# Second norm's scaling and modulation on ScalarE, key transposes after the next projection

## Chip, cores and metric

The kernel runs on one core of one Trainium2 chip. The metric is device time of one execution in microseconds (us), the median of several runs. Engines: PE is TensorE (PEld its weight loads), DVE is VectorE, ACT is ScalarE, POOL is GpSimd, SP issues the DMAs.

## What is computed

One layer of a decoder trunk over 1024 tokens of 1024 channels, in float32:

```python
mod = silu(c) @ w_ada + b_ada                  # sh1, sc1, g1, sh2, sc2, g2
h   = rms_norm(x, g_pre_mix) * (1 + sc1) + sh1
proj = h @ w_in                                # u, v, q, k, val, qi, ki, wi
y_a = spatial_gating(gelu(u), gelu(v), ...)    # 4 groups x 128, chunks of 128 positions
q, k, q_idx, k_idx = partial_rope(...)
y_b = dsa_attention(q, k, val, q_idx, k_idx, wi)   # top 256 keys of an indexer, softmax
o   = concat(rms_norm(y_a), rms_norm(y_b)) @ w_out
x   = x + g1 * rms_norm(o, g_post_mix)
h2  = rms_norm(x, g_pre_ffn) * (1 + sc2) + sh2     # the second norm
f   = square(relu(h2 @ w_ff1)) @ w_ff2
x   = x + g2 * rms_norm(f, g_post_ffn)
```

## The kernel before

The 1024 tokens are worked in 8 blocks of 128 (`j`), in two halves of 512 (`hh = j // 4`). Every matrix product is made of three passes: each float32 operand is split into a high part (rounded to the PE's fast float32 format, written by ACT) and a low part (source minus high part, by DVE or POOL), and high x high, high x low and low x high are summed in PSUM.

The order of instructions on each engine is not written by hand. The program is traced in source order, which gives each instruction a priority; `stage(n)` sets the priority of what follows. A planner that runs ahead of time with its own estimates of durations then takes, for each engine, the first instruction in priority that it reckons ready, and fixes that order. On the chip each engine runs its list strictly in this order and waits at semaphores. Tiles come from pools: tiles with one tag share `bufs` buffers, and a tile's first writer waits until the last reader of the tile that had the buffer before.

**Keys, end of stage 1 and stage 2 (L349 to L373).** For each block `j`: `proj` multiplies the block's normed rows by the 328 columns wC1 (keys, index key, index weights, values): 24 matmuls into one PSUM bank. Blocks 0 and 1 use tag `mm`, blocks 2 and 3 `lg`, blocks 4 to 7 `mm` again, which has two buffers. ACT copies the result out: `kv` (L361, each head twice), `WI` (L362), `VV` (L364); the bank is free after that. `rope` rotates `kv` on POOL (L314 to L317). PE transposes the three heads (`dup_T`, L322) into a `tr` bank; ACT copies them to `KS` and `KI` (L370, L371), and DVE subtracts there to get low parts (L372, L373). `kv` has two buffers. `modulate(1, ...)` (L287 to L294) makes the normed rows of blocks 4 to 7 out of channels x tokens tiles, at `j == 1` and `j == 2`: DVE L291, ACT L293 (high part), POOL or DVE L294 (low part). Stage 3 begins with `qi_proj` (L421), 512 columns wide, with the weights `wC0`, which take over buffers of `wC1` as block 7's projection has read them.

**Second norm, stage 8 (L912 to L931, `h2_block` L875).** For each block: load `x` (4 buffers) and the first half of `o`; `oproj` (24 matmuls, L795 to L797) into an `mm` bank; ACT squares it with a sum (L921); DVE and POOL make the reciprocal root (`rstd_of`: DVE L98, POOL power L99); DVE scales by it and the gate row (L924, L925), adds `x` (L926); the result is stored. Then the second norm: ACT squares the row with a sum (L928), `rstd_of` again, DVE scales the row (L930), and `h2_block` transposes its 8 channel blocks in two halves of four (L886). The first half is modulated (times `G2`, plus `SH2`, one number per channel) by four ACT instructions (L889), the second half by one DVE product (L892) and one POOL sum (L894). For the first 512 tokens two `split`s follow (ACT L863, DVE L864). For the others come differences for a fast matrix product of seven instead of eight sub-products: `t1` (DVE L903, L904), POOL L907 and L909, and four splits into `HB[1]`, `TT3` and `TT2`. Stage 9 then multiplies by `w_ff1`: the products of its first two weight tiles need `HB[0]` alone at first (L1012 and before), and then `T1` and `B22`, which are the two halves of `HB[1]` and need all four of its blocks (L1020, L1021; the matmuls are at L974 to L976).

Of the kernel before, what the change touches and what calls it, by code (L numbers as in the profile page):

```python
# [9 lines left out]
F32 = mybir.dt.float32  # L10
# [5 lines left out]
AF = mybir.ActivationFunctionType  # L16
OP = mybir.AluOpType
PSUM = bass.MemoryType.PSUM

P = 128  # L20
# [17 lines left out]
def trunk(ctx, tc, x, c, positions, w_ada, b_ada, g_pre_mix, w_in, g_sgu_v, w_spatial, b_spatial,  # L38
          g_out_sgu, g_out_attn, w_out, g_post_mix, g_pre_ffn, w_ff1, w_ff2, g_post_ffn, out):
    nc = tc.nc  # L40
    V, A, G, T = nc.vector, nc.scalar, nc.gpsimd, nc.tensor
# [5 lines left out]
    def nm(s):  # L47
        uid[0] += 1
        return f"{s}_{uid[0]}"
# [13 lines left out]
    def p_mm():  # L63
        return ps.tile([P, 512], F32, tag="mm", name=nm("mm"))

    def p_tr():
        return ps.tile([P, 512], F32, tag="tr", name=nm("tr"), bufs=3)
# [4 lines left out]
    def ct(shape, dt, name):  # L72
        return cst.tile(shape, dt, tag=name, name=name)

    def push(name, side="left"):
        st = ExitStack()
        return st, st.enter_context(tc.tile_pool(name=name, bufs=1, side=side, reuse_waits="tile"))

    def stage(n):
        tc.cur_priority = n * 100000  # L80
# [15 lines left out]
    def rstd_of(dst, ss, n):  # L96
        w = ss.shape[-1]
        V.tensor_scalar(dst, ss, 1.0 / n, EPS, op0=OP.mult, op1=OP.add)  # L98
        G.tensor_tensor(dst, dst, mhalf[:, :w], op=OP.pow)  # L99

    mid_stack, mid = push("mid")
    KS = mid.tile([P, 2, S], F32R, name="KS")
# [8 lines left out]
    KI = kp.tile([P, S], F32R, name="KI")  # L111
    t0_stack, t0 = push("t0")
# [174 lines left out]
    def modulate(hh, ks=range(KD), tok=slice(0, 512)):  # L287
        for k in ks:
            g, sh = G1[:, k:k + 1], SH1[:, k:k + 1]
            f = t0.tile([P, 512], F32, tag="hf", name=nm("hf"), bufs=2)[:, :tok.stop - tok.start]  # L290
            V.tensor_scalar(f, xT[hh][:, k, tok], g, sh, op0=OP.mult, op1=OP.add)  # L291
            hi = hT[hh][:, 0, k, tok]
            A.activation(hi, xT[hh][:, k, tok], AF.Identity, scale=g, bias=sh)  # L293
            (G if k % 4 in (1, 3) else V).tensor_tensor(hT[hh][:, 1, k, tok], f, hi.bitcast(F32), op=OP.subtract)  # L294

    def proj(p, j, wt, n, ks=range(KD)):
        h, t = hT[j // 4], (j % 4) * P
        first = None
        for k in ks:
            lh, ll = h[:, 0, k, t:t + P], h[:, 1, k, t:t + P]  # L300
            mm = T.matmul(p[:, :n], lh, wt[k][:, 0, :n], start=k == 0, stop=False)  # L301
            first = first or mm
            T.matmul(p[:, :n], lh, wt[k][:, 1, :n], start=False, stop=False)  # L303
            T.matmul(p[:, :n], ll, wt[k][:, 0, :n], start=False, stop=k == KD - 1)  # L304
        return first
# [13 lines left out]
    def dup_T(p, t, heads):  # L319

        for i, h in enumerate(heads):
            T.transpose(p[:, i * P:(i + 1) * P], t[:, h].rearrange("p w e -> p (w e)"), ident)  # L322
# [23 lines left out]
        pre_norm(j)  # L346
    stage(2)
    modulate(0, range(4, KD))
    for j in range(NB):  # L349
        if j == 1:  # L350
            modulate(1, tok=slice(0, 256))
        if j == 2:
            modulate(1, tok=slice(256, 512))
        if j < 4:
            p = p1[j]
            proj(p, j, wC1, 328, range(4, KD))
        else:
            p = p_mm()
            proj(p, j, wC1, 328)
        kv = t0.tile([P, 3, 2, 64], F32, tag="kv", name=nm("kv"), bufs=2)  # L360
        A.activation(kv, p[:, :192].rearrange("p (h e) -> p h e", h=3)[:, :, None, :].to_broadcast([P, 3, 2, 64]), AF.Copy)  # L361
        A.activation(WI[:, j], p[:, 192:200], AF.Copy, scale=float(8.0 ** -0.5) * 0.125)  # L362
        vv = p[:, 200:328].rearrange("p (h e) -> p h e", h=2)
        A.activation(VV[:, j], vv, AF.Copy)  # L364
        rope(kv.rearrange("p h w e -> p (h w e)"), j, 6, kp)
        pt = p_tr()
        dup_T(pt, kv, range(3))
        s = slice(j * P, (j + 1) * P)
        pt3 = pt[:, :384].rearrange("p (h t) -> p h t", h=3)
        A.activation(KS[:, :, s], pt3[:, 0:2], AF.Copy)  # L370
        A.activation(KI[:, s], pt3[:, 2], AF.Copy)  # L371
        V.tensor_tensor(KS[64:128, :, s], pt3[64:128, 0:2], KS[64:128, :, s].bitcast(F32), op=OP.subtract)  # L372
        V.tensor_tensor(KI[64:128, s], pt3[64:128, 2], KI[64:128, s].bitcast(F32), op=OP.subtract)  # L373

    def q_stack(pool, q, grp, qs):

# [98 lines left out]
    G2 = ct([P, 8], F32, "G2")  # L475
    SH2 = ct([P, 8], F32, "SH2")
# [56 lines left out]
    for cc in range(2):  # L533
        wt = w_chunk(w_in, [(0, C_U + 256 * cc, 256), (256, C_V + 256 * cc, 256)])
        for j in range(NB):
            p = p_mm()
# [38 lines left out]
    for b in range(2, NB):  # L575
        f, i = ct([P, 14], F32, f"self{b}"), ct([P, 3], I32, f"seli{b}")
# [285 lines left out]
    def split(hi, lo, src, eng):  # L862
        A.activation(hi, src, AF.Copy)  # L863
        eng.tensor_tensor(lo, src, hi.bitcast(F32), op=OP.subtract)  # L864
# [7 lines left out]
    rs2 = ct([P, NB], F32, "rs2")  # L872
    HB = {}

    def h2_block(j, y):  # L875
        t = (j % 4) * P
        hh = j // 4
        if hh not in HB:
            HB[hh] = hm.tile([P, 2, KD, 512], F32R, tag="hm", name=nm("hb"))
        f = y.rearrange("p (k t) -> p k t", k=KD)  # L880
        for half in range(2):
            ks = slice(half * 4, half * 4 + 4)
            p = p_tr()
            for i in range(4):
                k = half * 4 + i
                T.transpose(p[:, i * P:(i + 1) * P], y[:, k * P:(k + 1) * P], ident)  # L886
            if half == 0:
                for i in range(4):
                    A.activation(f[:, i, :], p[:, i * P:(i + 1) * P], AF.Identity, scale=G2[:, i:i + 1],  # L889
                                 bias=SH2[:, i:i + 1])  # L890
            else:
                V.tensor_tensor(f[:, ks], p.rearrange("p (k t) -> p k t", k=4), G2[:, ks, None].to_broadcast([P, 4, P]),  # L892
                                op=OP.mult)
                G.tensor_tensor(f[:, ks], f[:, ks], SH2[:, ks, None].to_broadcast([P, 4, P]), op=OP.add)  # L894
        tk = slice(t, t + P)
        if hh == 0:
            for half in range(2):
                ks = slice(half * 4, half * 4 + 4)
                split(HB[0][:, 0, ks, tk], HB[0][:, 1, ks, tk], f[:, ks], V)
            return  # L900
        b11 = [HB[0][:, q, 0:4, tk].bitcast(F32) for q in range(2)]
        t1 = l2.tile([P, 4, P], F32, tag="t1", name=nm("t1"), bufs=1)
        V.tensor_tensor(t1, f[:, 0:4], b11[0], op=OP.subtract)  # L903
        V.tensor_tensor(t1, t1, b11[1], op=OP.subtract)  # L904
        split(HB[1][:, 0, 0:4, tk], HB[1][:, 1, 0:4, tk], t1, V)
        split(HB[1][:, 0, 4:8, tk], HB[1][:, 1, 4:8, tk], f[:, 4:8], V)
        G.tensor_tensor(f[:, 0:4], f[:, 4:8], f[:, 0:4], op=OP.subtract)  # L907
        split(TT3[:, 0, :, tk], TT3[:, 1, :, tk], f[:, 0:4], V)
        G.tensor_tensor(f[:, 4:8], f[:, 4:8], t1, op=OP.subtract)  # L909
        split(TT2[:, 0, :, tk], TT2[:, 1, :, tk], f[:, 4:8], V)  # L910

    wo = w_chunk(w_out, [(0, 512, 512)], gout)  # L912
    for j in range(NB):
        xt = l2.tile([P, D], F32, tag="x", name=nm("x"), bufs=4)
        nc.sync.dma_start(xt, x2d[j * P:(j + 1) * P, :])
        o0 = l2.tile([P, 512], F32, tag="o0", name=nm("o0"), bufs=2)
        nc.sync.dma_start(o0, o0_dram[j * P:(j + 1) * P, :])
        p = p_mm()
        oproj(p, j, wo)
        x1 = l2.tile([P, D], F32, tag="x1", name=nm("x1"), bufs=2)  # L920
        A.activation(x1[:, 0:512], p, AF.Square, accum_out=sso[:, j, 1:2])  # L921
        V.tensor_tensor(rso[:, j:j + 1], sso[:, j, 0:1], sso[:, j, 1:2], op=OP.add)
        rstd_of(rso[:, j:j + 1], rso[:, j:j + 1], D)
        V.scalar_tensor_tensor(x1[:, 0:512], o0, rso[:, j:j + 1], g1b[:, 0:512], op0=OP.mult, op1=OP.mult)  # L924
        V.scalar_tensor_tensor(x1[:, 512:], p, rso[:, j:j + 1], g1b[:, 512:], op0=OP.mult, op1=OP.mult)  # L925
        V.tensor_tensor(x1, x1, xt, op=OP.add)  # L926
        nc.sync.dma_start(out2d[j * P:(j + 1) * P, :], x1)
        A.activation(xt, x1, AF.Square, accum_out=ss2[:, j:j + 1])  # L928
        rstd_of(rs2[:, j:j + 1], ss2[:, j:j + 1], D)
        V.tensor_scalar(xt, x1, rs2[:, j:j + 1], None, op0=OP.mult)  # L930
        h2_block(j, xt)  # L931
    l2_stack.close()

# [69 lines left out]
    for pi in range(NF):  # L1003
        raw = load_w1(pi)
        AW[pi] = {key: wsplit(raw[key], G) for key in raw}
        for fi in range(2):
            p = bank()
# [3 lines left out]
            p = bank()  # L1011
            product(p, AW[pi][fi, 1], B21)  # L1012
            f = F0[pi, fi] = dtile()
# [3 lines left out]
    for pi in range(NF):  # L1017
        for fi in range(2):
            p = bank()
            product(p, AW[pi][fi, 0], T1, stop=False)  # L1020
            product(p, AW[pi][fi, 1], B22, start=False)  # L1021
            f = part[pi, fi]
# [7 lines left out]
    for k in range(4):  # L1030
        t = fd.tile([P, 512], F32, tag="s", name=nm("t4"), bufs=4)
# [245 lines left out]
```

## Time and profile before

| | |
|---|---|
| median of 3 runs | 1256.06 us (1253.9 to 1257.73) |
| profiled execution | 1255.87 us, of which span 1254.1 us |
| mean granted TensorE clock | 0.961 of full |
| PE / DVE / ACT / POOL busy | 93% / 70% / 53% / 18% |

The span goes from the first to the last instruction of the profiled execution; the rest of its time lies around it. Times within the rows further down count from the span's start. A busy share is the share of a stretch in which the engine has an instruction under way. Matmuls are pipelined: the distance of two starts, not the duration, is what one costs.

### The profile page before, as it was taken

To read this page: it belongs to the slowest core of one execution; us is meant where nothing else is said; L and a number is where in the kernel's file an instruction comes from. 1 tells how busy PE (TensorE), PEld (TensorE's weight loads), DVE (VectorE), ACT (ScalarE), POOL (GpSimd) and SP (SyncE) were. 2 spreads that over 40 slices of the span, in tenths; PEclk is the share of its full clock that TensorE was granted. 3 is DMA by queue.
4 is the path that set the end of the run, shared out by engine and by line. 5 is a ranking of instruction groups with operands and counts; after the bars stand their busy time and mean duration, and the time that the engine had idled before them with its cause. 6 is when DMAs were issued, how large, how long until landed. Compare 5 with 4: busy or idle time off the path is not lost.

```text
span 1254.1 us, 16871 instructions
## 1 busy us (share of the span) xinstructions
PE 1169.4 (93%) x5785; PEld 987.7 (79%) x5785; DVE 876.2 (70%) x1782; ACT 661.9 (53%) x1402; POOL 222.9 (18%) x312
## 2 busy tenths in 40 slices
PE   4889979899699999899899999999999999999997
PEld 4877757688588998887677888888887888888886
DVE  6833998957697566627998875656648756876568
ACT  4544668772167755635525465555544554445452
POOL 3574702544300000013620000000000000000001
PEclk9889978899798999999999999999999999999999
DMA  9421200201002044446315753435459355533335
GB/s 344 146 67 43 68 1 18 85 22 55 1 9 68 26 152 160 168 136 226 126 43 185 269 192 127 161 126 175 151 201 353 118 177 182 198 98 101 102 95 207
DMA packets 80239, 162.41 MB, mean 130 GB/s; under 512 B 7724, under 2 KB 32920, under 8 KB 80152
## 3 DMA queue, kind: packets, MB, share of 16 engines
q1 hardware_dynamic: 80136, 161.33, 38.1%
q8 instruction: 45, 0.74, 0.2%
q14 instruction: 42, 0.34, 0.1%
q10 hardware_dynamic: 16, 0.00, 0.0%
HBM read 119.36 MB, written 41.94 MB: 129 GB/s over the span
## 4 chain that ended last, share of the span: by engine, by line
PE 60%; DVE 7%; issue 3%; DMA 1%; POOL 1%; ACT 1%; DVEq 0%; POOLq 0%; SPq 0%; ACTq 0%
PE lg L1157 9%; PE tr L1157 9%; PE mm L1157 6%; PE mm L743 5%; PE lg L974 3%; PE lg L975 3%; PE lg L976 3%; PE tr L974 3%; PE tr L976 3%; PE tr L975 3%; PE tr L757 2%; PE lg L718 2%; PE mm L974 2%; PE mm L975 2%; PE mm L976 2%
## 5 line engine op out<-in xcount | busy, mean ns | idle before, releaser
L863 ACT ACTIVATE w<-rx 128x512 fp32r<-128x512 f32 x112 | 70.6, 630 | 147.3 <-PE lg L1157 66.7
L1157 PE MATMUL tr<-w,w 128*128 128x512 f32 x504 | 133.8, 391 | 2.4 <-DVE w L864 2.4
L1157 PE MATMUL lg<-w,w 128*128 128x512 f32 x504 | 133.7, 391 | 0.0
L301 PE MATMUL mm<-w,hT 128*128 128x512 f32 (+1 forms) x288 | 113.2, 394 | 7.9 <-ACT hT L293 3.4
L864 DVE TENSOR_TENSOR w<-rx,w 128x512 fp32r<-128x512 f32 x112 | 77.4, 691 | 60.5 <-ACT w L863 60.3
L1193 POOL TENSOR_TENSOR rsf<-rsf,mhalf 128x1 f32<-128x1 f32 x8 | 6.0, 751 | 604.4 <-DVE rsf L1192 604.4
L1157 PEld LDWEIGHTS tr<-w,w 128*128 128x128 f32 x504 | 95.0, 189 | 22.5 <-DVE w L864 2.8
L304 PE MATMUL mm<-w,hT 128*128 128x512 f32 (+1 forms) x288 | 111.4, 388 | 1.0 <-POOL hT L294 1.0
L303 PE MATMUL mm<-w,hT 128*128 128x512 f32 (+1 forms) x288 | 111.7, 388 | 0.0
L1157 PEld LDWEIGHTS lg<-w,w 128*128 128x128 f32 x504 | 95.1, 189 | 19.7
L1157 PE MATMUL mm<-w,w 128*128 128x512 f32 x336 | 94.5, 392 | 0.0
L743 PEld LDWEIGHTS mm<-VV,pT 128*128 128x128 f32 x576 | 75.3, 199 | 4.5 <-ACT pT L738 2.5
L743 PE MATMUL mm<-VV,pT 128*128 128x64 f32 x576 | 76.3, 277 | 1.0 <-ACT pT L738 1.0
L1157 PEld LDWEIGHTS mm<-w,w 128*128 128x128 f32 x336 | 63.4, 189 | 13.2
L301 PEld LDWEIGHTS mm<-w,hT 128*128 128x128 f32 x288 | 56.2, 195 | 18.6 <-ACT hT L293 3.6
L864 DVE TENSOR_TENSOR w<-b,w 128x512 fp32r<-128x512 f32 x96 | 65.9, 687 | 3.6 <-ACT w L863 3.6
L864 DVE TENSOR_TENSOR w<-s,w 128x512 fp32r<-128x512 f32 x56 | 38.2, 690 | 37.6 <-ACT w L863 37.4
L304 PEld LDWEIGHTS mm<-w,hT 128*128 128x128 f32 x288 | 55.7, 194 | 10.4 <-POOL hT L294 1.3
L863 ACT ACTIVATE w<-b 128x512 fp32r<-128x512 f32 x96 | 59.3, 618 | 7.1 <-DMA b<-in_w_ff_dram 7.1
L303 PEld LDWEIGHTS mm<-w,hT 128*128 128x128 f32 x288 | 56.2, 195 | 8.5
L718 PE MATMUL lg<-KS,qs 128*128 128x512 f32 (+5 forms) x192 | 53.3, 388 | 10.2 <-DVE qs L383 8.8
L722 ACT ACTIVATE L<-L,mxs 128x128 f32<-128x128 f32 (+7 forms) x64 | 49.2, 770 | 20.4 <-DVE mxs L719 20.4
(357 smaller groups left out, 2988.6 us busy)
## 6 DMA issues: line engine op xcount, KB each, us to landing
rx<-x_scratch SPq DMA_DIRECT2D x56, 512.0 KB, 3.6
x_scratch<-d SPq DMA_DIRECT2D x108, 256.0 KB, 3.0
ada<-in_w_ada_dram SPq DMA_DIRECT2D x48, 512.0 KB, 5.7
raw<-in_w_ff_dram SPq DMA_DIRECT2D x32, 512.0 KB, 3.9
b<-in_w_ff_dram SPq DMA_DIRECT2D x32, 512.0 KB, 4.4
x<-in_x_dram SPq DMA_DIRECT2D x16, 512.0 KB, 5.5
raw<-in_w_in_dram SPq DMA_DIRECT2D x8, 512.0 KB, 3.7
raw<-in_w_in_dram SPq DMA_DIRECT2D x16, 256.0 KB, 2.9
```

What stands on the lines that cost most here:

```text
L301: mm = T.matmul(p[:, :n], lh, wt[k][:, 0, :n], start=k == 0, stop=False)
L303: T.matmul(p[:, :n], lh, wt[k][:, 1, :n], start=False, stop=False)
L304: T.matmul(p[:, :n], ll, wt[k][:, 0, :n], start=False, stop=k == KD - 1)
L718: T.matmul(pl, QS[b, grp][:, q, h4 * P:(h4 + 1) * P], KS[:, grp, c0:c0 + cw], start=q == 0, stop=q == 1)
L722: ex = A.activation(L, L, AF.Exp, scale=-1.0, bias=top, accum_out=sms[:, b, h:h + 1])
L743: mm = T.matmul(po[:, o:o + 64], e[:, (si * 2 + h2) * P:(si * 2 + h2 + 1) * P], VV[:, s0 + si, grp], start=first, stop=pair == 1 and s0 + ...
L863: A.activation(hi, src, AF.Copy)
L864: eng.tensor_tensor(lo, src, hi.bitcast(F32), op=OP.subtract)
L974: ms.append(T.matmul(p, a[:, 0, k], b[:, 0, k], start=start and k == 0, stop=False, skip_group_check=more))
L975: ms.append(T.matmul(p, a[:, 0, k], b[:, 1, k], start=False, stop=False, skip_group_check=more))
L976: ms.append(T.matmul(p, a[:, 1, k], b[:, 0, k], start=False, stop=stop and k == 3, skip_group_check=more))
L1157: ms.append(T.matmul(p, x[:, qa, t * P:(t + 1) * P], y[:, qb], start=start and n == 0, stop=stop and n == 2, skip_group_check=more))
```

## The change

The keys' transposes of a block, with the copies and subtractions behind them, go into a function `keys_T` that is called one block later: after the next block's projection, copies and rotation. `kv` gets a third buffer. In the second norm, the row's scaling goes from DVE to ACT, and the second half of the channels is modulated like the first, by four ACT instructions, in place of the DVE product and the POOL sum.

```diff
+    keys = []
+
+    def keys_T(j, kv):
+
+        pt = p_tr()
+        dup_T(pt, kv, range(3))
+        s = slice(j * P, (j + 1) * P)
+        pt3 = pt[:, :384].rearrange("p (h t) -> p h t", h=3)
+        A.activation(KS[:, :, s], pt3[:, 0:2], AF.Copy)
+        A.activation(KI[:, s], pt3[:, 2], AF.Copy)
+        V.tensor_tensor(KS[64:128, :, s], pt3[64:128, 0:2], KS[64:128, :, s].bitcast(F32), op=OP.subtract)
+        V.tensor_tensor(KI[64:128, s], pt3[64:128, 2], KI[64:128, s].bitcast(F32), op=OP.subtract)
+
     for j in range(NB):
...
-        kv = t0.tile([P, 3, 2, 64], F32, tag="kv", name=nm("kv"), bufs=2)
+        kv = t0.tile([P, 3, 2, 64], F32, tag="kv", name=nm("kv"), bufs=3)
...
         rope(kv.rearrange("p h w e -> p (h w e)"), j, 6, kp)
-        pt = p_tr()
-        dup_T(pt, kv, range(3))
...
+        if keys:
+            keys_T(*keys.pop(0))
+        keys.append((j, kv))
+    keys_T(*keys.pop(0))
...
-            if half == 0:
-                for i in range(4):
-                    A.activation(f[:, i, :], p[:, i * P:(i + 1) * P], AF.Identity, scale=G2[:, i:i + 1],
-                                 bias=SH2[:, i:i + 1])
-            else:
-                V.tensor_tensor(f[:, ks], p.rearrange("p (k t) -> p k t", k=4), G2[:, ks, None].to_broadcast([P, 4, P]),
-                                op=OP.mult)
-                G.tensor_tensor(f[:, ks], f[:, ks], SH2[:, ks, None].to_broadcast([P, 4, P]), op=OP.add)
+            for i in range(4):
+                k = half * 4 + i
+                A.activation(f[:, k, :], p[:, i * P:(i + 1) * P], AF.Identity, scale=G2[:, k:k + 1],
+                             bias=SH2[:, k:k + 1])
...
-        V.tensor_scalar(xt, x1, rs2[:, j:j + 1], None, op0=OP.mult)
+        A.activation(xt, x1, AF.Copy, scale=rs2[:, j:j + 1])
         h2_block(j, xt)
```

## Rows read from the trace of the kernel before

**Rows 1.** The page: busy time of each engine, and the chain by engine.
```profile
PE 1169.4 (93%) x5785; PEld 987.7 (79%) x5785; DVE 876.2 (70%) x1782; ACT 661.9 (53%) x1402; POOL 222.9 (18%) x312
...
PE 60%; DVE 7%; issue 3%; DMA 1%; POOL 1%; ACT 1%; DVEq 0%; POOLq 0%; SPq 0%; ACTq 0%
```

**Rows 2.** Busy by stretch: length, then busy (xcount) PE, PEld, DVE, ACT, POOL; clock, DMA.
```profile
65.00:80.00 15.00, 9.79 (x50) 9.15 (x49) 7.82 (x17) 4.44 (x19) 8.80 (x19) 0.77 0.12 35
...
150.00:330.00 180.00, 163.04 (x715) 132.79 (x714) 139.03 (x445) 108.47 (x305) 65.00 (x103) 0.91 0.11 32
...
640.00:1254.00 614.00, 602.69 (x2646) 495.79 (x2645) 422.99 (x680) 296.40 (x530) 5.98 (x8) 0.99 0.49 166
```

**Rows 3.** The same view for the second norm's stage and its end.
```profile
606.00:640.10 34.10, 26.20 (x112) 21.03 (x111) 33.18 (x39) 19.09 (x39) 21.76 (x17) 0.88 0.22 78
...
566.70:640.10 73.40, 64.29 (x297) 52.27 (x296) 64.00 (x92) 42.87 (x93) 41.15 (x35) 0.94 0.39 137
564.70:640.10 75.40, 66.29 (x306) 53.96 (x305) 65.97 (x93) 43.29 (x95) 41.15 (x35) 0.94 0.41 145
```

**Rows 4.** PE in order of time: start, us, instruction, [idle before <-releaser].
```profile
61.95 0.49 PE L322 MATMUL tr<-ident,kv 128*128 128x128 f32 x3
...
71.35 0.55 PE L322 MATMUL tr<-ident,kv 128*128 128x128 f32 x3 [3.94 <-POOL kv L317]
73.16 0.64 PE L301 MATMUL mm<-w,hT 128*128 128x328 f32 x1 [1.26 <-ACT VV L364]
73.60 0.48 PE L303 MATMUL mm<-w,hT 128*128 128x328 f32 x1
73.87 0.48 PE L304 MATMUL mm<-w,hT 128*128 128x328 f32 x1
...
80.48 0.42 PE L301 MATMUL mm<-w,hT 128*128 128x328 f32 x1 [0.34 <-ACT VV L364]
80.73 0.31 PE L303 MATMUL mm<-w,hT 128*128 128x328 f32 x1
80.88 0.31 PE L304 MATMUL mm<-w,hT 128*128 128x328 f32 x1
...
84.18 0.40 PE L301 MATMUL mm<-w,hT 128*128 128x512 f32 x1
```

**Rows 5.** ACT in order of time, the copies of keys and of block 4.
```profile
71.93 0.38 ACT L370 ACTIVATE KS<-tr 128x256 fp32r<-128x256 f32 x1 [4.05 <-PE tr L322]
...
72.37 0.50 ACT L361 ACTIVATE kv<-mm 128x384 f32<-128x384 f32 x1
```

**Rows 6.** POOL in order of time: end of block 2's rotation, last low half.
```profile
71.01 0.28 POOL L317 TENSOR_TENSOR kv<-ra,rb 128x48 f32<-128x48 f32 x1
...
72.51 0.73 POOL L294 TENSOR_TENSOR hT<-hf,hT 128x256 fp32r<-128x256 f32 x1 [0.23 <-DVE hf L291]
```

**Rows 7.** PE in order of time, its two long waits in the second norm.
```profile
622.99 3.80 PE L886 MATMUL tr<-ident,x 128*128 128x128 f32 x16 [4.99 <-DVE x L930]
...
638.67 0.80 PE L974 MATMUL lg<-hb,w 128*128 128x512 f32 x1 [2.66 <-ACT hb L863]
```

**Rows 8.** Single lines, whole run: xcount, ns min/median/max, first and last start.
```profile
L930 DVE TENSOR_SCALAR x<-x,rs x8: 741/754/1773, 570.7 to 623.4; 128x1024 f32<-128x1024 f32 x8
L892 DVE TENSOR_TENSOR x<-tr,G x8: 678/679/686, 576.6 to 627.5; 128x512 f32<-128x512 f32 x8
L894 POOL TENSOR_TENSOR x<-x,SH x8: 1041/1481/1952, 577.4 to 630.1; 128x512 f32<-128x512 f32 x8
L904 DVE TENSOR_TENSOR t<-t,hb x4: 678/1215/1778, 613.2 to 636.2; 128x512 f32<-128x512 f32 x4
L928 ACT ACTIVATE x<-x x8: 1047/1062/1065, 566.7 to 615.6; 128x1024 f32<-128x1024 f32 x8
```

**Rows 9.** ACT in order of time: eight modulations of 128 channels in a row.
```profile
574.85 2.91 ACT L889 ACTIVATE x<-tr,SH,G 128x128 f32<-128x128 f32 x8 [0.61 <-PE tr L886]
```

**Rows 10.** DVE in order of time: block 1's scaling behind POOL's power.
```profile
571.52 0.15 DVE L98 TENSOR_SCALAR rs<-ss 128x1 f32<-128x1 f32 x1
572.33 0.75 DVE L930 TENSOR_SCALAR x<-x,rs 128x1024 f32<-128x1024 f32 x1 [0.65 <-POOL rs L99]
```

More of the change, by code (lines that the diff above doesn't have):

```diff
@@ L365, in trunk @@
         rope(kv.rearrange("p h w e -> p (h w e)"), j, 6, kp)
-        pt = p_tr()
-        dup_T(pt, kv, range(3))
[L368 to L373, printed above, removed]
+        if keys:
+            keys_T(*keys.pop(0))
+        keys.append((j, kv))
+    keys_T(*keys.pop(0))
     def q_stack(pool, q, grp, qs):
```

## Prediction

> **What bounds the kernel now.** Read first the busy shares and the chain that ended last: TensorE (PE) is busy 93% of the span and carries 60% of the chain; VectorE (DVE) is at 70%, ScalarE (ACT) at 53% [rows 1]. The reader is to see that a gain can only come where PE stands still or runs at its lower clock, and that ACT has room on average; an average says nothing of a stage. So the second view is busy time by stretch. From 640 us to the end PE works 602.7 of 614 us and nothing of the change lies there [rows 2]: whatever is saved earlier arrives at the end whole, unless the stage between takes it back. From 150 to 330 us PE is at 163 and DVE at 139 of 180 us [rows 2], all of it behind the projections of stage 3, so a shift goes through, if the planner keeps its order.
>
> The change touches two stretches. **65 to 80 us**: PE is busy 9.8 of 15 us at a granted clock of 0.77 [rows 2]. **566 to 640 us** (second norm): after 606 us DVE is busy 33.2 of 34.1 us, ACT 19.1, PE 26.2 [rows 3]. There PE waits 4.99 us for the scaled rows of L930, a DVE instruction, and 2.66 us for the last split tile [rows 7]. In this stage DVE is the bound.
>
> **The keys.** The transposes of a block's keys already stand far behind later projections: those of block 0 run at 61.95 us, with block 4's projection on both sides [rows 4], since the planner places by readiness. The new order in the source alone moves little. What binds is a buffer: with two kv tiles, block 4's copy out of PSUM (L361, 72.37 us) may not run before block 2's keys are transposed (71.35 us) [rows 4, 5], and block 6's projection may not have its bank before that copy. The third kv buffer breaks this tie. It adds no instruction and takes 1.5 KB per partition of a pool that is closed after the stage; no DMA is moved, and nothing is moved past a queue that issues one.
>
> Removed for certain are the two waits for a bank behind ACT's copy of VV: 1.26 us at 73.16 and 0.34 us at 80.48 [rows 4]: 1.6 us. Open is the stall ahead of them, 3.94 us until POOL has rotated block 2's keys (L317, done at 71.29 us) [rows 4, 6], and what it leaves behind: matmuls at a distance of 0.27 us (73.60, 73.87), at full clock 0.15 us (80.73, 80.88) [rows 4], some 20 of them, 2.4 us. The granted clock falls from 2.4 to 1.2 GHz behind the stall. ACT is idle from 67.88 us (71.93 less 4.05 [rows 5]); block 4 could be copied out then, in the 0.8 us from 72.37 to 73.16, so that block 6 starts at 68.7 us, if the planner puts it ahead of the transposes that come ready at 71.29 us. It can't end before the last low half of its rows (L294 on POOL, 72.51 + 0.73 us [rows 6]), 73.3 us; block 7 takes 24 x 0.15 = 3.6 us more, and stage 3 starts at about 77.4 us instead of 84.18 [rows 4]: 6.8 us at the most. If the planner keeps the transposes ahead, 1.6 us is all. Below that it may fall to nothing where other work then stands in front. I take **2.5 us**: the certain part and a quarter of the stall. Before, the order was forced by the buffer, so it doesn't tell which one the planner prefers; the low end is nearer as PE needs the transposes first wherever both look ready.
>
> **The second norm.** Removed from DVE: 8 scalings (L930, 0.75 us median, up to 1.77) and 8 products (L892, 0.68 us); from POOL: 8 sums (L894, 1.48 us) [rows 8]. That is 8 x 0.75 + 8 x 0.68 = 11.4 us of DVE and 11.8 us of POOL. DVE also gets back part of what it loses while POOL works: the same 128x512 subtraction L904 takes 0.68 to 1.78 us [rows 8]. Added to ACT: 8 scalings of 128x1024, nearest row the Square L928 of the same shape, 1.06 us [rows 8], 8.5 us; and 32 activations of 128x128 at 2.91 / 8 = 0.364 us each (L889 [rows 9]), 11.6 us. ACT: 20.1 us more.
>
> The sum goes by the stage. ACT has 42.9 us of work in the 73.4 us from 566.7 to 640.1; then it has 63.0 us. DVE falls from 66.0 us (of 75.4) to 54.6 [rows 3]. So the bound passes from DVE to ACT, and the question is how full ACT can be: the stage keeps its length at 63.0 / 73.4 = 86%. DVE as the bound came to 66.0 / 75.4 = 87.5% over the stage and to 97% at its end [rows 3]. ACT at 87.5% needs 72.0 us (1.4 us gained), at 97% 64.9 us (8.5 us). I take 90%, 70.0 us, **3.4 us** gained: ACT has work of several blocks to choose from, as DVE had, but each block now comes to it three times (square, scaling, modulation), and the planner's order is fixed beforehand. What is late next is again the last block's split tile ahead of PE's restart at 638.67 us [rows 7]. The path of one block is hardly longer: the scaling 1.06 for 0.75 us, the second half's modulation 4 x 0.364 = 1.46 us for 0.68 + 1.48 us and a handover [rows 8, 9]. Cover: POOL's and DVE's removed work hides nothing; the added ACT work lies beside PE's oproj and the first products of stage 9, and without that cover costs its 20.1 us less DVE's 11.4, 8.7 us.
>
> The trace has an ACT instruction with two per-channel operands at 0.364 us for 128 columns [rows 9], and DVE with POOL at 2.16 us for 512. The Trainium skill (ScalarE: Activation LUTs, Rules for kernel authors) speaks against the edit: multiplications and additions belong on VectorE, not on ScalarE. By that rule alone the sum would be a loss; for the scaling the rows agree (1.06 against 0.75 us), for the modulation they don't, as half of the work it replaces is POOL's. The skill (SBUF — State Buffer, Who interferes with whom) also has a DVE instruction with two SBUF inputs contend with a GpSimd one that reads SBUF; the spread of L904 [rows 8] agrees, and this adds DVE time back that I don't count.
>
> **Sum.** The profiled execution took 1255.87 us (span 1254.1 and 1.8 around it), 0.2 under the median. 1255.87 - 2.5 - 3.4 = 1250.0 us.
>
> **Rivals.**
> *ACT becomes a worse bound than DVE was (slower).* Each scaling needs the square of its own block, the small sum on DVE and POOL's power. DVE itself waited 0.65 us there after a 0.15 us instruction (L930 at 572.33 us [rows 10]), 0.8 us in all. If the planner puts L930 straight behind L928 on ACT, with copies and splits queued behind it, 8 x 0.8 = 6.4 us of ACT go idle: 69.4 us at 87.5% is 79.3 us, 5.9 us longer than 73.4. With the certain 1.6 us of the keys 1260.2 us, without it 1261.8. It decides where ACT is less than 86% full. For it: ACT sits in the in-order chain three times. Against: blocks overlap, and DVE did reach 97%. Chance 0.19.
> *Nothing to be measured.* The keys give only the bank waits, ACT reaches 87.5%: 1255.87 - 1.6 - 1.4 = 1252.9 us. For it: the new bound is nearly as high as the old. This holds too where the reordered keys do nothing, as they already stand behind later projections. Chance 0.31.
> *Both ends good.* Block 6 goes ahead of the transposes, 6.8 us, and ACT takes 3.4 to 8.5 us less: 1240.6 to 1245.7 us. Chance 0.12.
>
> **How the numbers follow.** The forecast, 0.38, reaches from 1246 to 1252 us. A measurement of this kernel can tell about 0.3%, 3.8 us, from no change: faster ends at 1252.3, slower begins at 1259.8 us. Faster: 0.38 less a small part, and the good end, 0.48. Same: the second rival and that part, 0.33. Slower: the first, 0.19. A new plan also shuffles orders that have nothing to do with the change, which is why no case is a point. The range of 8 in 10 goes from 1243 to 1260 us; left out are half of the good end and most of the slower case beyond 1260.
>
> **What would show it.** Keys: kv of block 4 on ACT ahead of block 2's KS copy; no 1.26 us wait for VV; first 512-wide matmul of stage 3 at 77 to 82.5 us instead of 84.18. If PE still stands some 4 us before a kv transpose, the low end held. Norm: ACT 86% full or more from 567 us to PE's restart, DVE under 80%; the restart 3 to 4 us earlier when counted from the start of stage 8. The prediction is wrong if ACT waits on POOL's power (L99) at each scaling, if PE waits for a bank of oproj behind ACT, or if the stretch between 100 and 560 us changes length by more than 2 us.

## The result and the profile after

| | before | after |
|---|---|---|
| median of 5 runs | 1254.46 us (1253.6 to 1257.73) | 1246.09 us (1243.53 to 1247.74) |
| profiled execution, of which span | 1255.87 us, 1254.1 us | 1243.53 us, 1241.8 us |
| mean granted TensorE clock | 0.961 | 0.971 |

The changed kernel takes 0.9924 of the time before, 95% interval 0.9905 to 0.9943: 8.4 us less by the medians, 9.5 us by this ratio, where 1250.0 us (5.9 less than the profiled execution) was forecast and 1243 to 1260 given as the range. The profiled execution of after is the fastest of its five, so the two traces differ by 12.3 us at their ends; the size of the gain is taken from the medians, the traces say where it lies.

The page of the kernel after, busy time of each engine and the chain by engine, to be held against [rows 1]:

```profile
PE 1161.0 (93%) x5785; PEld 979.4 (79%) x5785; DVE 861.9 (69%) x1766; ACT 680.6 (55%) x1442; POOL 212.0 (17%) x304
...
PE 59%; DVE 6%; issue 3%; ACT 3%; DMA 2%; POOL 0%; SPq 0%; DVEq 0%; POOLq 0%; ACTq 0%
```

ACT works 18.7 us more, DVE 14.3 and POOL 10.9 us less. ACT's share of the chain rises from 1% to 3%. PE's busy time falls too, by 8.4 us with the same 5785 matmuls: part of what was saved is matmuls at the lower clock, and not idle time.

PE of the kernel after in order of time: the start, the duration, the instruction, and the idle time before it with its releaser. The rows up to 77.15 us answer to [rows 4], the rest to [rows 7]:

```profile
60.71 0.49 PE L322 MATMUL tr<-ident,kv 128*128 128x128 f32 x3
...
68.56 0.55 PE L322 MATMUL tr<-ident,kv 128*128 128x128 f32 x3 [2.24 <-POOL kv L317]
68.88 0.41 PE L301 MATMUL mm<-w,hT 128*128 128x328 f32 x1
69.14 0.31 PE L303 MATMUL mm<-w,hT 128*128 128x328 f32 x1
69.29 0.31 PE L304 MATMUL mm<-w,hT 128*128 128x328 f32 x1
...
77.15 0.39 PE L301 MATMUL mm<-w,hT 128*128 128x512 f32 x1
...
610.78 1.09 PE L895 MATMUL tr<-ident,x 128*128 128x128 f32 x8 [0.45 <-ACT x L935]
...
612.82 0.65 PE L895 MATMUL tr<-ident,x 128*128 128x128 f32 x4 [0.95 <-ACT x L935]
...
614.74 0.66 PE L895 MATMUL tr<-ident,x 128*128 128x128 f32 x4 [1.26 <-ACT x L898]
...
616.65 0.80 PE L979 MATMUL tr<-hb,w 128*128 128x512 f32 x1 [1.26 <-ACT x L898]
...
628.18 0.50 PE L979 MATMUL lg<-hb,w 128*128 128x512 f32 x1 [1.68 <-ACT hb L872]
```

The third set of transposes, block 2's, is still the one that PE waits for, and still for POOL's rotation, but 2.24 us instead of 3.94. Block 6's projection (L301 at 68.88) follows at once: the 1.26 us wait for a bank is gone. Its matmuls stand 0.15 us apart (69.14, 69.29) instead of 0.27. The first 512-wide matmul comes at 77.15 instead of 84.18 us. In the second norm the 4.99 us wait for DVE's scaled row has turned into four small waits for ACT, 3.9 us together, and the restart on the split tile comes at 628.18 instead of 638.67 us.

Busy time by stretch: length, then busy us (count) of PE, PEld, DVE, ACT, POOL, then the granted clock, DMA share and GB/s. First of the kernel before, two pieces of the keys' stretch and stage 8 from its first square to PE's restart:

```profile
70.00:75.00 5.00, 2.39 (x10) 2.15 (x11) 2.97 (x9) 1.18 (x5) 4.54 (x13) 0.68 0.00 0
75.00:80.00 5.00, 5.00 (x25) 4.87 (x24) 0.16 (x1) 0.75 (x3) 0.14 (x1) 0.64 0.00 0
...
559.50:638.70 79.20, 70.09 (x327) 57.13 (x325) 65.63 (x95) 43.21 (x97) 41.02 (x37) 0.96 0.45 160
```

The same view of the kernel after; the last row begins at the first square of L933:

```profile
65.00:80.00 15.00, 12.76 (x83) 11.92 (x82) 9.38 (x22) 9.46 (x34) 14.46 (x27) 1.00 0.25 71
...
551.20:628.20 77.00, 69.36 (x327) 56.42 (x325) 48.67 (x79) 60.94 (x137) 29.86 (x29) 0.98 0.47 164
558.10:628.20 70.10, 62.47 (x297) 50.69 (x295) 45.63 (x74) 59.55 (x132) 29.31 (x27) 0.98 0.42 145
```

From 65 to 80 us PE is busy 12.8 of 15 us instead of 9.8 [rows 2]. From 70 to 80 us the granted clock was 0.68 and 0.64, the mean of pieces at 1.2 and at 2.4 GHz; after, it is 1.00 from 65 to 80 us. Stage 8 is 2.2 us shorter (79.2 to 77.0), with DVE's work down by 17.0 us and ACT's up by 17.7: the fullest engine beside PE is now ACT.

Counted along the trace, after is ahead of before by 7.0 us at the start of stage 3, by 8.3 us at the first square of stage 8 (551.21 for 559.54 us), by 10.5 us at PE's restart and by 10.0 us at the first product with TT (655.65 for 665.62 us). Of the first 7.0 us, 1.2 are there before block 0's transposes already (60.71 for 61.95 us). This mark lies between 60.71 and 63.45 us in all kernels below and goes with no edit, so the keys account for 5.8 us in this pair of traces.

### The profile page after: what moved, and what is told of

Read it like the earlier page. It is cut to its first block, busy times and chain, and to the rows that moved or that the text cites. A ratio compares the mean times of both kernels' runs of the same rounds, so it can differ in the third digit from the quotient of the medians.

```text
span 1241.8 us, 16873 instructions
## 1 busy us (share of the span) xinstructions
PE 1161.0 (93%) x5785; PEld 979.4 (79%) x5785; DVE 861.9 (69%) x1766; ACT 680.6 (55%) x1442; POOL 212.0 (17%) x304
## 4 chain that ended last, share of the span: by engine, by line
PE 59%; DVE 6%; issue 3%; ACT 3%; DMA 2%; POOL 0%; SPq 0%; DVEq 0%; POOLq 0%; ACTq 0%
PE tr L1162 8%; PE lg L1162 8%; PE mm L1162 5%; PE mm L752 4%; PE lg L980 3%; PE lg L981 3%; PE lg L979 3%; PE tr L981 3%; PE tr L980 3%; PE tr L979 3%; PE tr L766 2%; PE lg L727 2%; PE mm L981 2%; PE mm L980 2%; PE mm L979 2%
## 5 line engine op out<-in xcount | busy, mean ns | idle before, releaser
L301 PE MATMUL mm<-w,hT 128*128 128x512 f32 (+1 forms) x288 | 112.0, 390 | 4.4 <-ACT hT L293 3.7
L301 PEld LDWEIGHTS mm<-w,hT 128*128 128x128 f32 x288 | 55.2, 192 | 15.1 <-ACT hT L293 3.9
L304 PEld LDWEIGHTS mm<-w,hT 128*128 128x128 f32 x288 | 54.9, 191 | 10.0 <-POOL hT L294 0.6
L303 PEld LDWEIGHTS mm<-w,hT 128*128 128x128 f32 x288 | 55.3, 192 | 8.5
```

## The experiments

The theories. *The buffer*: what binds the keys is the two kv tiles, and the order in the source does nothing. Rival: the order is needed as well, or alone. *The stage's bound*: the second norm gains because DVE, with POOL, was its bound and hands work to ACT; rivals: only one of the two edits gives the gain, or POOL's sums are what cost the time and it doesn't matter where the work goes.

**The two halves of the change, each alone.** keys_only takes the diff without its two edits in stage 8, norm_only these two alone.

> The keys' part alone (keys_T one block later, third kv buffer); second norm as before. Theory A: the keys' part carries most of the gain, since stage 3 began 7.0 us earlier in the changed kernel (77.15 against 84.18 us) and stage 8 8.3 us earlier: 6 to 8 us faster than before, first 512-wide matmul at about 77 us. Rival B: the two parts share the gain as predicted, keys 2.5 us: 1.6 to 3 us faster. Rival C: most of what stands at stage 8 is a shuffled plan between, then the start of stage 3 moves by 7 us but the end by less than 4.

> The second norm's part alone (scaling and all modulation on ACT); keys as before. Theory A: 1.5 to 2.5 us faster, since from the first square of oproj to PE's restart on the split tiles the changed kernel took 77.0 us and before 79.1; with ACT 85% full in that stretch. Prediction's term: 3.4 us. Rival: nothing or a loss, the whole gain being that of the keys.

Measured: keys_only 0.9943 (0.9929 to 0.9956), 7.2 us less; norm_only 0.9973 (0.996 to 0.9986), 3.4 us less. Together 10.6 us, where both at once gave 9.5 (0.9924): additive as far as the intervals can tell, so no sign that one half takes the other's gain.

**The keys, cut in two.** buffer_only keeps the old order:

```diff
-        kv = t0.tile([P, 3, 2, 64], F32, tag="kv", name=nm("kv"), bufs=2)
+        kv = t0.tile([P, 3, 2, 64], F32, tag="kv", name=nm("kv"), bufs=3)
```

order_only takes `keys_T` and its later call from the diff and leaves `bufs=2`.

> Only the third kv buffer; transposes in the old source order. Theory A: the buffer does it, because block 2's copy out of PSUM no longer waits for block 0's transposes and goes ahead of the eight modulations on ACT: copy of block 2 at about 59 us instead of 65.6, 6 to 8 us faster, as keys_only. Rival: the new source order is needed as well: less than 3 us.

> Only the new source order, kv with two buffers as before. Theory A: nothing, within 2 us of before, copy of block 2 still at about 65 us; with two buffers a copy two blocks on still waits for transposes that now come later in priority, so a loss of 1 to 2 us is possible. Rival: the order does it, 6 to 8 us faster.

Measured: buffer_only 0.9944 (0.9931 to 0.9957), 7.1 us less, the same as keys_only; order_only 1.0003 (0.9993 to 1.0013), nothing. PE and ACT of order_only in order of time:

```profile
71.06 0.90 PE L322 MATMUL tr<-ident,kv 128*128 128x128 f32 x3 [4.47 <-POOL kv L317]
73.23 0.64 PE L301 MATMUL mm<-w,hT 128*128 128x328 f32 x1 [1.26 <-ACT VV L377]
...
65.35 0.48 ACT L374 ACTIVATE kv<-lg 128x384 f32<-128x384 f32 x1
```

Both waits stand as in [rows 4]. The whole gain of the keys is one number in the source, the third buffer.

**Which wait the buffer removes.** In the prediction block 4's copy waits for block 2's transposes. There is an earlier pair of the same kind, which I had not looked at: block 2's copy waits for block 0's transposes. ACT of the kernel before:

```profile
61.17 4.13 ACT L293 ACTIVATE hT<-xT,SH,G 128x256 fp32r<-128x256 f32 x8
...
65.63 0.48 ACT L361 ACTIVATE kv<-lg 128x384 f32<-128x384 f32 x1
```

And the same of the kernel after:

```profile
59.24 0.47 ACT L374 ACTIVATE kv<-lg 128x384 f32<-128x384 f32 x1
...
62.72 4.05 ACT L293 ACTIVATE hT<-xT,SH,G 128x256 fp32r<-128x256 f32 x8 [1.78 <-DVE xT L285]
...
68.10 0.50 ACT L374 ACTIVATE kv<-mm 128x384 f32<-128x384 f32 x1
...
69.14 0.38 ACT L357 ACTIVATE KS<-tr 128x256 fp32r<-128x256 f32 x1 [0.31 <-PE tr L322]
```

Before, block 0's transposes come at 61.95 us, when the eight modulations of L293 have begun on ACT (61.17), and block 2's copy stands behind them, at 65.63. With a third buffer it runs at 59.24, ahead of them. Block 4's copy has moved as well: at 68.10, before block 2's KS copy (69.14), where it stood behind it [rows 5]. To tell the two apart, the tiles were tagged by hand, with one buffer for each tag. free2 gives block 2 a buffer of its own and lets block 4 wait for block 2 as before; free4 the reverse:

```diff
+        kv = t0.tile([P, 3, 2, 64], F32, tag="kv" + "abcbcbcb"[j], name=nm("kv"), bufs=1)   # free2
+        kv = t0.tile([P, 3, 2, 64], F32, tag="kv" + "ababcbcb"[j], name=nm("kv"), bufs=1)   # free4
```

> Three kv buffers handed out by hand so that every block waits for the same earlier block as before, except block 2, which has a buffer of its own and doesn't wait for block 0's transposes (block 4 still waits for block 2's). Theory A: this one wait carries the gain of the keys: 5 to 7 us faster, block 2's copy at about 60 us, PE's stall on block 2's rotation shortened from 3.94 to about 2 us, and no lower clock behind it. Prediction's mechanism (block 4's copy behind block 2's transposes is what binds): nothing, under 1 us.

> The same, but only block 4 is freed: it doesn't wait for block 2's transposes; block 2 still waits for block 0's. Theory A: 1.3 to 2.5 us faster (the wait for block 4's bank at 73.2 us goes), block 2's copy still at about 65.6 us. Prediction's mechanism: 1.6 us if PE keeps the transposes ahead, up to 6.8 us if block 6 goes ahead of them.

Measured: free2 0.9966 (0.9954 to 0.9978) and free4 0.9966 (0.9954 to 0.9978), 4.3 us less each by the ratio (2.8 to 5.8), under the 5 to 7 expected of free2 and over the 1.3 to 2.5 expected of free4. Each wait alone is worth a part of the 7.1 us (5.4 to 8.7) of the third buffer; whether the two parts add up the intervals leave open. PE of free2, then a stretch of it by the columns above:

```profile
69.12 0.55 PE L322 MATMUL tr<-ident,kv 128*128 128x128 f32 x3 [1.98 <-POOL kv L317]
70.93 0.42 PE L301 MATMUL mm<-w,hT 128*128 128x328 f32 x1 [1.26 <-ACT VV L364]
```

```profile
70.00:75.00 5.00, 4.07 (x17) 4.07 (x18) 2.98 (x9) 0.88 (x5) 4.13 (x10) 0.66 0.00 0
```

The stall is halved, as in the changed kernel, but the wait for the bank stays, and behind the two the clock falls (0.66). The same of free4:

```profile
67.13 0.42 PE L301 MATMUL mm<-w,hT 128*128 128x328 f32 x1 [0.17 <-ACT VV L364]
...
72.11 0.49 PE L322 MATMUL tr<-ident,kv 128*128 128x128 f32 x3
73.47 0.48 PE L304 MATMUL mm<-w,hT 128*128 128x328 f32 x1 [0.87 <-POOL hT L294]
```

```profile
75.00:80.00 5.00, 4.63 (x17) 4.38 (x18) 1.27 (x4) 4.02 (x13) 4.19 (x12) 0.50 0.01 3
```

Here block 6's projection does go ahead of block 2's transposes, the case that the prediction priced at 6.8 us. It runs into the low halves of its own rows (L294 on POOL) in several small waits (0.17 to 0.87 us), and from 75 to 80 us the clock is at 1.2 GHz (0.50). The transposes of block 0, those of block 2 and the first 512-wide matmul, from PE's rows in order of time of each kernel (us), and the granted clock from block 2's transposes to stage 3. The last three rows are the changed keys with other edits of the second norm, told of below:

| | block 0 | block 2 | stage 3 | 0 to 2 | 2 to stage 3 | clock |
|---|---|---|---|---|---|---|
| before | 61.95 | 71.35 | 84.18 | 9.40 | 12.83 | 0.73 |
| order_only | 60.95 | 71.06 | 83.46 | 10.11 | 12.40 | 0.77 |
| free2 | 61.68 | 69.12 | 81.02 | 7.44 | 11.90 | 0.86 |
| free4 | 61.34 | 72.11 | 81.79 | 10.77 | 9.68 | 0.65 |
| buffer_only | 63.45 | 70.31 | 78.88 | 6.86 | 8.57 | 1.00 |
| keys_only | 62.03 | 69.50 | 78.10 | 7.47 | 8.60 | 1.00 |
| after | 60.71 | 68.56 | 77.15 | 7.85 | 8.59 | 1.00 |
| keys_mod_dve | 62.97 | 70.38 | 78.99 | 7.41 | 8.61 | 1.00 |
| keys_mod_act | 61.31 | 69.15 | 79.32 | 7.84 | 10.17 | 0.83 |
| after_mod_dve | 60.93 | 68.77 | 78.89 | 7.84 | 10.12 | 0.83 |

Block 2's earlier copy shortens the first interval by 1.6 to 2.5 us, block 4's the second; the third buffer has both, 5.8 to 6.8 us in all where the clock stayed up, 4.2 to 4.3 us in the two traces where it fell. Of the 4.24 us that the second interval loses from before to after, 1.6 us are the two bank waits; the other 2.6 lie where the matmuls no longer run at the lower clock. That the clock stays up is not a sure part of the gain. keys_mod_act has the keys of the changed kernel and one wait nearly as long, and its clock falls; PE in order of time, then a stretch by the columns above:

```profile
69.15 0.55 PE L322 MATMUL tr<-ident,kv 128*128 128x128 f32 x3 [2.26 <-POOL kv L317]
```

```profile
70.00:75.00 5.00, 5.00 (x26) 4.99 (x25) 3.28 (x9) 0.91 (x5) 4.62 (x13) 0.66 0.00 0
```

For free2 the intervals give 2.9 us and for free4 1.8, the ratios 4.3. In free4's trace another 3.2 us lie between stage 3 and the first square of stage 8 (472.1 for 475.4 us); but this execution is the fastest of its twelve, and the stretch takes 472.1 to 475.7 us over all the kernels here, with and without edits: how much of free4's gain is the freed buffer's is open.

**The second norm, cut in two.** scale_only and mod_only take one edit of the stage each:

```diff
-        V.tensor_scalar(xt, x1, rs2[:, j:j + 1], None, op0=OP.mult)            # scale_only
+        A.activation(xt, x1, AF.Copy, scale=rs2[:, j:j + 1])
...
-            if half == 0:                                                       # mod_only
...
+            for i in range(4):
+                k = half * 4 + i
+                A.activation(f[:, k, :], p[:, i * P:(i + 1) * P], AF.Identity, scale=G2[:, k:k + 1],
+                             bias=SH2[:, k:k + 1])
```

> Second norm: only the row's scaling goes to ACT; the second half of the modulation stays on DVE and POOL; keys as before. Theory A: DVE loses 6 to 8 us of work in a stage that it bounds, 1 to 2 us faster. Rival: the scaling stands in ACT's in-order chain ahead of the transposes and PE waits for it instead: nothing or 1 us slower.

> Second norm: only the second half of the channels is modulated on ACT; scaling stays on DVE; keys as before. Theory A: this takes POOL's 12 us away as well, whose sums hold up DVE, so it carries most of the 3.4 us that the norm's part measured: 2 to 3.5 us faster. Rival: the two edits are needed together, each alone gives under 1 us.

Measured: scale_only 1.0007 (0.9995 to 1.0019), nothing; mod_only 0.9971 (0.9959 to 0.9983), 3.6 us less, as much as both edits. Busy by stretch from the first square of stage 8 to PE's restart, of scale_only:

```profile
559.70:636.50 76.80, 69.18 (x327) 56.49 (x325) 60.11 (x86) 49.78 (x103) 39.60 (x35) 0.98 0.48 165
```

Then of mod_only:

```profile
559.20:636.80 77.60, 70.74 (x326) 56.97 (x324) 55.56 (x87) 53.28 (x129) 30.74 (x29) 0.96 0.47 163
```

And of norm_only, both edits without the keys:

```profile
558.10:635.30 77.20, 69.62 (x327) 56.56 (x325) 48.70 (x79) 61.06 (x137) 29.94 (x29) 0.98 0.47 164
```

The same stage of before takes 79.2 us. In the traces of the kernels that leave it unedited (before and the five of the keys) it takes 78.0 to 79.1 us; the shortest is keys_only:

```profile
553.00:631.00 78.00, 70.01 (x327) 57.38 (x325) 64.86 (x95) 42.99 (x97) 40.63 (x36) 0.96 0.45 162
```

So all three lie below this spread, mod_only by little, and keys_mod_act (below), whose second norm is that of mod_only, takes 78.0 us: one trace doesn't size a gain of 1 or 2 us. scale_only has the shortest of the three, is 2.2 us ahead of before at the restart, and gives it back. PE and ACT of scale_only at the entry of the products with TT:

```profile
665.31 0.50 PE L974 MATMUL tr<-TT,w 128*128 128x512 f32 x1 [3.39 <-ACT c L1097]
...
664.14 0.63 ACT L863 ACTIVATE w<-raw 128x512 fp32r<-128x512 f32 x1 [1.08 <-DMA raw<-in_w_ff_dram]
664.68 0.58 ACT L1097 ACTIVATE c<-tr 128x512 f32<-128x512 f32 x1
```

The copy that frees a bank for PE (L1097) was put behind a split of the next weights, whose load had not landed; PE waits 3.39 us there, where it waits 0.69 us before, after and in mod_only. That order is the planner's; nothing of the edit asks for it. This mark comes at 665.31 us, 0.3 us earlier than before (665.62).

**The other end of the modulation.** mod_dve takes the sums from POOL and leaves the second half on DVE:

```diff
+                else:
+                    V.tensor_scalar(f[:, k, :], p[:, i * P:(i + 1) * P], G2[:, k:k + 1], SH2[:, k:k + 1],
+                                    op0=OP.mult, op1=OP.add)
```

> Second norm: the second half's modulation as four DVE instructions (times G2, plus SH2 in one) in place of the DVE product and the POOL sum; nothing goes to ACT; keys as before. Theory A: what the norm's part gains comes from taking POOL's 12 us of sums away, whose port use holds up DVE and which stand in each block's path: 2 to 3.5 us faster though DVE keeps its load. Rival: it comes from DVE's 5.4 us: nothing or slower, as four DVE instructions of 128 columns cost more than one of 512.

Measured: 0.9986 (0.9974 to 0.9997), 1.8 us less by the ratio. Busy in the stage, as above:

```profile
558.20:636.70 78.50, 69.18 (x326) 56.42 (x324) 65.31 (x118) 42.26 (x97) 32.49 (x29) 0.98 0.45 161
```

DVE's new instructions take more than those they replace (32, 11.0 us, for 8 products, 5.4 us), its total is the same (65.31 for 65.63 us), and still the kernel is a little faster: it seems that taking POOL's sums away is worth something by itself, if only just clear of nothing. How the gain of mod_only divides between POOL's sums and DVE's products stays open, as 1.8 us (0.4 to 3.3) and 3.6 us (2.1 to 5.1) overlap.

**Combinations, to look for a better kernel.** Against the changed kernel, keys_mod_act has the scaling back on DVE; keys_mod_dve has this and the second half's modulation as in mod_dve; after_mod_dve has the modulation alone so:

```diff
-        A.activation(xt, x1, AF.Copy, scale=rs2[:, j:j + 1])      # keys_mod_act, keys_mod_dve
+        V.tensor_scalar(xt, x1, rs2[:, j:j + 1], None, op0=OP.mult)
```

> The changed kernel with the row's scaling back on DVE. Theory A: the scaling's move is worth nothing (alone it measured nothing), so this equals the changed kernel: 9 to 10.5 us faster than before. Rival: with the modulation on ACT too, DVE's relief by the scaling counts: 1 to 2 us slower than the changed kernel.

> The keys' part, and the second half's modulation as four DVE instructions, scaling on DVE. Theory A: 9 to 11 us faster than before, the sum of the keys' 7 us and the modulation's 2 to 3.5 us. Rival: DVE, again the bound, gives less: 7 to 8 us.

> The changed kernel with the second half's modulation as four DVE instructions (scaling on ACT, no POOL sum): loads between the two engines evened out. Theory A: as good as the changed kernel or better by up to 3 us, ACT 70 to 75% full in the stage instead of 85%: 9 to 13 us faster than before. Rival: ACT's scaling in front of the transposes costs what it saves: 7 to 8 us.

Measured: keys_mod_act 0.9933 (0.9915 to 0.9951), keys_mod_dve 0.9944 (0.9928 to 0.996), after_mod_dve 0.9929 (0.9912 to 0.9946). None is faster than the changed kernel (0.9924). The scaling may stay on DVE at no cost that these intervals show. keys_mod_dve, for which 9 to 11 us were expected (7.0 measured), is no faster than the keys alone (0.9943): the 1.8 us of mod_dve aren't found again there; the differences among the three lie within their intervals, so no more is read from them.

## Why the prediction was right or wrong

**The time lies inside the range; one term was mis-sized, and the other came out by luck.** 1250.0 us was forecast, 1246.09 measured: inside the range, at the edge of the forecast case (1246 to 1252).

**The keys, 2.5 us forecast, 7 measured.** Right: the order in the source does nothing, the buffer binds; the 1.26 us wait and the 0.34 us wait go; the transposes of block 2 stay ahead of block 6, as the planner was reckoned to keep them; block 4's copy runs before block 2's KS copy. The step that failed is "If the planner keeps the transposes ahead, 1.6 us is all". It had two faults. First, only block 4's buffer was followed. The same tie between blocks 0 and 2 sent block 2's copy behind eight modulations on ACT, and its rotation came later too: POOL began it at 69.09 us before and at 66.01 after. The rotation did not wait for the copy itself, which was done at 66.11 us before. With the late copy the planner put two low halves ahead of the rotation on POOL, the second of them waiting for DVE; order_only and free4 have this order too, free2, buffer_only, keys_only and after do not. POOL of the kernel before:

```profile
68.36 0.76 POOL L294 TENSOR_TENSOR hT<-hf,hT 128x256 fp32r<-128x256 f32 x1 [0.88 <-DVE hf L291]
69.09 0.56 POOL L314 TENSOR_TENSOR ra<-kv,CS 128x96 f32<-128x96 f32 x1
```

The stall falls from 3.94 to 2.24 us and the transposes come 1.6 us nearer to block 0's; free2 has just this. Second, the 2.4 us of slow matmuls were hung on block 6 going ahead. In the changed kernel it doesn't go ahead, and the clock stays up all the same: block 6 starts right behind the transposes (68.88) and runs at full distance. 1.6 + 1.6 + 2.6 us make the 5.8 us of the trace; where the clock fell in spite of the third buffer (keys_mod_act, after_mod_dve) it is 4.2 to 4.3 us, so part of the 2.6 us does not come with the buffer for certain. The end of 6.8 us was about the right size by luck, for a wrong reason; where block 6 did go ahead (free4), the gain was 4.3.

What is late next is again POOL: the third transposes still wait 2.24 us for L317, since in POOL's order a weight split stands ahead of the rotation and a low half in its midst; the copy had been done since 59.71 us. POOL after, in order of time:

```profile
64.77 1.28 POOL L222 TENSOR_TENSOR w<-raw,w 128x512 fp32r<-128x512 f32 x1
66.01 0.56 POOL L314 TENSOR_TENSOR ra<-kv,CS 128x96 f32<-128x96 f32 x1
...
66.98 0.91 POOL L294 TENSOR_TENSOR hT<-hf,hT 128x256 fp32r<-128x256 f32 x1
```

**The second norm, 3.4 us forecast, 3.4 measured alone.** The bound passes to ACT as said: 59.55 of 70.1 us, 85%. That its fullness stayed under the 86% named as break-even, and the stage still gained, has one reason: ACT had less work than reckoned. Between these marks (first square of a row to the restart, 72.0 us before) ACT was busy 41.8 us before, so 20.1 more would be 61.9; the 63.0 of the prediction are counted to 640.1 us, past the restart. Measured were 59.55 us, 17.8 more: neighbours on ACT overlap, the groups of its instructions add up to 70.2 us there for 59.55 busy, 46.5 for 41.8 before. For 59.55 the break-even is 83%. So ACT was 85% full with a smaller work instead of 90% with the larger, and that the term agrees with the measured 3.4 us is luck: between these marks the trace is 1.9 us shorter, the restart came 2.2 us earlier in the stage, not 3 to 4, and where the rest of the 3.4 us lies the traces don't show. The prices were near: the scaling took 1.153 us (median) for 1.06 estimated.

Wrong was the share of the parts: the term counted the scaling on both sides, 8.5 us for ACT and 6.0 us off DVE, and it is worth nothing that was measured, alone (1.0007), beside the modulation (0.9971 without it, 0.9973 with it) or in the full change (0.9933 and 0.9924). DVE's relief was 17.0 us, not 11.4. DVE in stage 8 before: busy us and mean ns of a group, then the idle time before it:

```profile
L926 DVE TENSOR_TENSOR x<-x,x 128x1024 f32<-128x1024 f32 x8 | 11.0, 1380 | 0.0
L930 DVE TENSOR_SCALAR x<-x,rs 128x1024 f32<-128x1024 f32 x8 | 8.0, 1002 | 1.5 <-POOL rs L99 1.4
L892 DVE TENSOR_TENSOR x<-tr,G 128x512 f32<-128x512 f32 x8 | 5.4, 681 | 0.0
L904 DVE TENSOR_TENSOR t<-t,hb 128x512 f32<-128x512 f32 x4 | 4.9, 1222 | 0.0
```

The same of the kernel after, where L931 and L909 are the lines L926 and L904 of before:

```profile
L931 DVE TENSOR_TENSOR x<-x,x 128x1024 f32<-128x1024 f32 x8 | 9.7, 1222 | 0.1
L909 DVE TENSOR_TENSOR t<-t,hb 128x512 f32<-128x512 f32 x4 | 3.8, 958 | 0.1
```

2.0 us of the difference is that I took the median of L930 (0.75 us), where its sum goes by the mean (1.002 us, 8.0 us in all); against this mean the scaling on ACT (1.06 estimated) cost hardly more, so the rows spoke less clearly for DVE than the prediction said. The other 3.6 us (17.0 less 8.0 and 5.4) are instructions that stayed and became shorter in sum, as the two rows show. This is what the Trainium skill (SBUF — State Buffer, Who interferes with whom) led one to look for, and the prediction left it out of the sum. mod_only agrees: POOL's sums gone, 5.4 us of products gone, and DVE 10.1 us down (65.63 to 55.56). Two more runs bear on it. In mod_dve POOL's sums are gone and DVE keeps the modulation, and DVE's other instructions take some 5 us less (65.31 less 11.0 for 65.63 less 5.4, and one instruction of about 1 us falls outside). In scale_only POOL's sums stay and 8.0 us of scaling are gone, but DVE is only 5.5 us down (65.63 to 60.11), so its other instructions took 2.5 us more. The relief goes with POOL's sums; but scale_only also shows that a new order by itself moves DVE's time by some 2 us, so POOL as the cause of all of it is argued, not shown.

**The rivals.** "ACT a worse bound" did not come, though its mechanism did, at two scalings early in the stage. ACT of the kernel after:

```profile
562.13 1.15 ACT L935 ACTIVATE x<-x,rs 128x1024 f32<-128x1024 f32 x1 [2.85 <-POOL rs L99]
...
565.17 1.15 ACT L935 ACTIVATE x<-x,rs 128x1024 f32<-128x1024 f32 x1 [0.85 <-POOL rs L99]
```

3.7 us of ACT in two waits instead of 0.8 us at each of eight; at the later blocks the planner had other work ahead of the scaling. "Nothing to be measured" was right about the order and wrong about the buffer. "Both ends good" gave 1240.6 to 1245.7 us; the keys came out at its end, the norm did not. Of the prediction's signs of being wrong none came: oproj's one wait is for DVE (1.07 us before, 1.13 after), not ACT, and the stretch between 100 and 560 us kept its length, as the sum needs: from the first 512-wide matmul to the first square of stage 8 it is 475.4 us before and 474.1 after.

## What to carry to other kernels

Where a tile's copy out of PSUM waits for an old buffer, follow every block through the pool, not only the one beside the longest wait: the buffer's price is also what its late copy stands behind on an in-order engine. Of a change that has a new order and a new buffer, try the buffer alone; with a planner that places by readiness, the order in the source moved nothing here. In the stage bound by DVE the move that freed two engines (product and sum) gained and the one that freed DVE alone did not. A mean, not a median, goes into a sum of durations.

## What the runs showed of the hardware

Whether the granted clock falls behind a short stall of PE made some 1.5 us of difference here. With one wait before block 2's transposes of 1.41, 1.96, 2.02 or 2.24 us (buffer_only, keys_mod_dve, keys_only, after) the clock stayed at 1.00 up to stage 3. With one wait of 2.26 or 2.27 us (keys_mod_act, after_mod_dve) part of the matmuls behind it ran at 1.2 GHz (0.83 on the mean), and from the transposes to stage 3 it took 10.17 and 10.12 us instead of 8.6, with no further wait. In free4 it fell behind four waits of 0.17 to 0.87 us. What decides it these runs don't show.

In the six kernels with two buffers (before, order_only, and the second norm's edits alone) PE waited 3.60 to 4.49 us, and the clock came to 0.73 to 0.77. The second wait, for the bank, is not what brought it down in before: over that wait it was at 1.2 GHz already, as this stretch by the columns above shows:

```profile
71.90:73.16 1.26, 0.00 (x1) 0.01 (x1) 1.17 (x4) 1.18 (x5) 1.03 (x2) 0.50 0.00 0
```

In order_only, norm_only, mod_only and mod_dve block 2's transposes, ahead of the second wait, ran slow already (0.84 to 0.90 us for 0.55). In free2, after 1.98 and then 1.26 us, it fell behind the second wait. free2 needs 3.3 us more than buffer_only from block 2's transposes to stage 3 (11.90 and 8.57), of which the bank waits are 1.6; the other 1.7 go with the lower clock.
